# A third attention unit turned by DMA after GpSimd lays it apart, with values and a convolution step moved

## The chip, the core and the metric

The kernel runs on one core of one Trainium2 chip. Five engines work side by side there: PE (TensorE, matrix products and transposes by an identity), DVE (VectorE), ACT (ScalarE), POOL (GpSimd) and SP (SyncE, which issues most DMAs). Each engine takes its instructions in a fixed order and starts one when what it waits for is there. The metric is the device time of the whole program in microseconds (us), lower is better. The inputs lie in the device's main memory, and so does the output.

## The reference, cut to what matters

Two layers; in each, a feed-forward block, a mixing block and a second feed-forward block. The change lies in the mixing block alone.

```python
h = rms_norm(x, mix_norm[l])
z = h @ w_in[l]                                   # 512 x 2304
q, k, v = ...                                     # 8 query heads, 2 key/value heads of 64
attn_out = sliding_window_attention(q, k, v, attn_sink[l])
conv_out = short_conv(z[..., V_END:CB_END], z[..., CB_END:CC_END], z[..., CC_END:CH_END], conv_w[l])
x = x + jnp.concatenate([attn_out, conv_out], axis=-1) @ w_out[l]
```

Attention works on blocks of 128 tokens: a block of queries sees its own block of keys and the one before. `short_conv(b, c, h)` is `b * conv3(c * h)`, a causal convolution over three tokens in each of 512 channels.

## The kernel before

**Layout.** Activations lie transposed, features on the 128 partitions and the 512 tokens along the row. Every float32 operand of a product is split into a high part (`wh`, `xh`, `ph`: ACT casts it) and a low part (`wl`, `xl`, `pl`: DVE subtracts the high part from the whole), and a product is high·high + high·low + low·high. One product of 128 output features (`group`, lines 302 to 325) is 8 slabs of 128 input features with 3 matmuls each: L318 (`wh`,`xh`), L319 (`wh`,`xl`), L321 (`wl`,`xh`). The call `between(k, hi, lo)` ahead of slab k lets other work of PE be put inside.

**The mixing block.** After keys, values and queries come 12 products for the convolution, one for each `step` from 6 to 17, in two pairs of channel blocks: two for C (`cc`, L1700), two for the convolved input (`ch`, L1707, and then taps and sums), two for B (L1720). Each product is followed by `go_on()`, which runs `attend(step)` and then asks for the split of later weights (`need_split`), which the scheduler may not place ahead of the instruction `last` that `attend` returned.

**The attention units.** There are eight, 4 heads by 128 queries each: units 0 to 3 are token blocks 0 to 3 of the first key/value head, units 4 to 7 those of the second. In the traces' names a unit is `block_head`: unit 1 is `1_0`, unit 2 is `2_0`, unit 3 is `3_0`, unit 4 is `0_1`, unit 5 is `1_1`. A unit has three stages, and the tables `SCORES_AT`, `TURN_AT` and `VALUES_AT` (lines 56 to 60) give each unit's step for them:

- *scores*: 8 matmuls (L1554, L1555); DVE adds the bias and takes the maximum (L1558); DVE negates it (`nm`, L1569); ACT takes the exponential of each head (L1575, it needs `nm`); DVE scales by the reciprocal of the sum (L1583, four instructions). Unit 2's stand at step 7.
- *turn*: the probabilities `p` are turned so that keys lie on the partitions, and split into `ph` (ACT, L1621) and `pl` (DVE, L1622). Units 0, 2, 4, 6 and 7 are turned by PE: 4 transposes for each block of keys (L1616) into a PSUM tile `pt`. Units 1, 3 and 5 (`SEND_AT`) are turned by DMA: `send` has ACT lay the two 16-bit halves of each word apart in a room of their own (`crossing`, L1590), SP issues a transposing DMA (L1592), and later `join` has ACT put the halves together again (L1601), once for each block of keys.
- *values*: 2 matmuls for each block of keys (L1633, L1634), ACT copies half of the result (L1636), DVE adds (L1639).

`INSIDE = (11, 4, 5)` puts unit 4's turn (4 transposes, it has one block of keys) inside the product of step 11, ahead of slab 5.

**A convolution channel's end** (lines 1709 to 1716): ACT scales `ch` twice (`cc`, `tap`), DVE adds the third tap (L1712, inputs `ch` and `tap`, both in SBUF), POOL adds and multiplies (L1715, L1716). Then comes `go_on()`.

**What sets the order.** The lists above give the order of the calls; a scheduler places the instructions on each engine by its own costs, so that DVE's and ACT's order can shift far from the code. Tiles of p share 8 buffers with the raw weights (`stock`).

Of the kernel before, what the change touches and what calls it, by code (L numbers as in the profile page):

```python
# [14 lines left out]
ALU = mybir.AluOpType  # L15
# [3 lines left out]
S = 512  # L19
# [35 lines left out]
STREAM_BACK_AT = {9: 0, 11: 1, 16: 2, 18: 3}  # L55
SCORES_AT = (5, 6, 7, 8, 9, 10, 12, 13)

SEND_AT = {7: 1, 9: 3, 11: 5}
TURN_AT = (6, 9, 8, 11, 10, 13, 14, 15)
VALUES_AT = (7, 10, 9, 12, 11, 14, 15, 16)  # L60
INSIDE = (11, 4, 5)
WARM = 3
XT_TAGS = ("sc", "aux", "aux", "mm", "sc", "sc", "aux", "aux")

# [11 lines left out]
def trunk_kernel(  # L76
# [23 lines left out]
    nc = tc.nc  # L100
# [31 lines left out]
    def f32(ap):  # L132
        return ap.bitcast(F32)

    def words(ap):

        return ap.bitcast(U16).rearrange("p (n two) -> p two n", two=2)
# [50 lines left out]
    def conv_of(l, k, c):  # L188
        at = 48 + 12 * l + 4 * k + c
        return par[:, at : at + 1]  # L190
# [1303 lines left out]
    def mix(l, norm, after):  # L1494
        q = [None] * NH

        mixed = [g8(f"m_{l}_{j}", F32, (P, KC // 2, S)) for j in range(2)]
# [37 lines left out]
        class Unit:  # L1535
# [49 lines left out]
            def send(self):  # L1585


                self.room = crossing[:, todo.index(self) // 2 % 2, :]
                halves = self.room.bitcast(U16).rearrange("p (two n) -> p two n", two=2)
                nc.scalar.copy(halves, words(self.p.rearrange("p h k -> p (h k)")))  # L1590
                self.turned = self.p.rearrange("p h k -> p (h k)").bitcast(U16)
                nc.sync.dma_start_transpose(  # L1592
                    self.turned.rearrange("p (c q) -> p c q", q=P),
                    halves.rearrange("p two n -> p (two n)"),
                )
# [11 lines left out]
            def turn(self):  # L1607

                self.pt = []
                for kb in range(self.lo // P, 2):  # L1610
                    if todo.index(self) in SEND_AT.values():
                        tp = self.join(kb)
                    else:
                        tp = psum("aux", [P, 4, P], f"pt_{self.name}_{kb}")
                        for h in range(4):
                            nc.tensor.transpose(  # L1616
                                tp[:, h, :], self.p[:, h, kb * P : (kb + 1) * P], ident
                            )
                    hi = g2(f"ph_{self.name}_{kb}", F32R, (P, 4, P))
                    lo = g2(f"pl_{self.name}_{kb}", F32R, (P, 4, P))  # L1620
                    nc.scalar.copy(hi, tp)  # L1621
                    last = nc.vector.tensor_sub(lo, tp, f32(hi))  # L1622
                    self.pt.append((kb, hi, lo))
                return last

# [17 lines left out]
        todo = [Unit(n, g) for g in range(NKV) for n in range(NT)]  # L1643
        crossing = g8(f"crossing_{l}", F32, (P, 2, 4 * 2 * P))

        def attend(step):

            done = None
            if step in SEND_AT:
                todo[SEND_AT[step]].send()  # L1650
            for at, stage in ((VALUES_AT, "values"), (TURN_AT, "turn"), (SCORES_AT, "scores")):
                if stage == "turn" and step + 1 == INSIDE[0]:
                    done = todo[VALUES_AT.index(step)].added
                    continue
                if step in at:
                    done = getattr(todo[at.index(step)], stage)() or done
            return done

        for j in range(NH // 2):
# [16 lines left out]
        step = 6  # L1676

        def product():

            def between(k, hi, lo):  # L1680
                if step == INSIDE[0] and k == INSIDE[2]:
                    todo[INSIDE[1]].turn()

            return group(norm.h, between, own=take_split(SPLIT_AHEAD - 1))

# [10 lines left out]
        for pair in range(2):  # L1696
            cs = []
            for j in range(2):
                c = g2(f"cc_{l}_{pair}_{j}")
                nc.vector.tensor_mul(c, product(), inv2)  # L1700
                cs.append(c)
                go_on()
            ys = []
            for j in range(2):
                c = 2 * pair + j
                u = g2(f"ch_{l}_{pair}_{j}")
                nc.vector.tensor_mul(u, product(), cs[j])  # L1707
                y = cs[j]
                nc.scalar.activation(y, u, AF.Copy, scale=conv_of(l, 2, c))
                tap = g2(f"tap_{l}_{c}")  # L1710
                nc.scalar.activation(tap[:, 1:], u[:, : S - 1], AF.Copy, scale=conv_of(l, 1, c))
                nc.vector.scalar_tensor_tensor(  # L1712
                    tap[:, 2:], u[:, : S - 2], conv_of(l, 0, c), tap[:, 2:], op0=ALU.mult, op1=ALU.add
                )
                nc.gpsimd.tensor_add(y[:, 1:], y[:, 1:], tap[:, 1:])  # L1715
                nc.gpsimd.tensor_mul(y, y, norm.inv)  # L1716
                ys.append(y)
                go_on()
            for j in range(2):
                last = nc.vector.tensor_mul(mixed[1][:, 2 * pair + j, :], product(), ys[j])  # L1720
                go_on()
                if step == 17:
                    with tc.issue_after(state["turned"]):
                        ops.make("b11")
# [60 lines left out]
```

## Time and profile before

| | |
|---|---|
| time, median of 3 runs | 1626.22 us (1626.18 to 1626.57) |
| the profiled execution, its own time | 1626.19 us |
| its span, first to last instruction | 1624.4 us |
| PE busy | 1615.4 us (99%) |
| DVE busy | 1376.7 us (85%) |
| ACT busy | 1178.1 us (73%) |
| POOL busy | 216.5 us (13%) |
| steps 6 to 12 of the first layer's mixing block | 368.6 to 416.6 us of the span |
| the same stretch of the second layer | 1171.4 to 1219.3 us |

The profile is one execution. Its page gives busy times and the chain of work that ended last; views of the trace give instructions in order of time (start, length, engine, line, what is written and read, and in brackets how long the engine stood idle before it and what ended that), groups of instructions, and who waited for whom. PE counts as busy from the start of one matmul to the modelled end of the last that overlaps it, so its waits are best read from the distance of one start to the next: 0.227 us between products of 512 columns that wait for nothing. Instructions on ACT and DVE overlap too: the next starts about 0.1 us before the end of the one before.

### The profile page before, as it was taken

What the parts mean: (1) busy time and instruction counts of PE and PEld (TensorE: products, weight loads), DVE (VectorE), ACT (ScalarE), POOL (GpSimd) and SP (SyncE); (2) the same over time, 40 slices, a digit from 0 to 9 for tenths busy, and PEclk for the clock granted to TensorE, in tenths of its full rate; (3) what the DMA queues carried; (4) which work ended last, traced back from release to release, by engine and by line L of the source; (5) the groups of instructions that cost most, each with busy time, mean ns of one, the idle gap of its engine ahead of it and who ended that gap; (6) DMA issues with size and microseconds to landing.
All of it is one profiled execution on the core that took longest, in us unless ns stands there. A gap on an engine that the chain in (4) does not pass through costs nothing.

```text
span 1624.4 us, 21158 instructions
## 1 busy us (share of the span) xinstructions
PE 1615.4 (99%) x7571; PEld 1349.4 (83%) x7571; DVE 1376.7 (85%) x1788; ACT 1178.1 (73%) x1511; POOL 216.5 (13%) x191
## 2 busy tenths in 40 slices
PE   9999999999999999999999999999999999999998
PEld 7888888888898888888888888888888988888887
DVE  7978798988899977798998777989688998678997
ACT  6677777857766677778866777788586767878665
POOL 1211111001211111111011111110012111111121
PEclk9999999999999999999999999999999999999999
DMA  9999989822597698999767999998136978999892
GB/s 270 212 232 209 220 207 226 233 59 78 143 227 175 177 225 214 218 214 225 218 144 182 224 215 226 215 221 217 42 91 156 233 149 219 225 223 222 241 230 72
DMA packets 306031, 313.92 MB, mean 193 GB/s; under 512 B 125501, under 2 KB 188549, under 8 KB 305925
## 3 DMA queue, kind: packets, MB, share of 16 engines
q1 hardware_dynamic: 265412, 230.90, 50.1%
q0 software_dynamic: 40048, 81.27, 29.3%
q8 instruction: 59, 0.97, 0.2%
q14 instruction: 48, 0.39, 0.1%
q10 hardware_dynamic: 464, 0.40, 0.1%
HBM read 264.29 MB, written 2.10 MB: 164 GB/s over the span
## 4 chain that ended last, share of the span: by engine, by line
PE 98%; DVE 1%; DMA 0%; SPq 0%; issue 0%; ACT 0%; DVEq 0%
PE x L842 27%; PE y L842 13%; PE x_s L842 9%; PE acc L318 7%; PE acc L319 7%; PE acc L321 7%; PE w L842 7%; PE y_s L842 5%; PE x_m L827 3%; PE w_s L842 3%; PE y_m L827 1%; PE y_e L842 1%; PE acc L699 1%; PE x_e L842 1%; PE w_m L827 1%; PE sc L1555 0%
## 5 line engine op out<-in xcount | busy, mean ns | idle before, releaser
L228 DVE TENSOR_TENSOR wl<-raw,wh 128x1024 fp32r<-128x1024 f32 (+1 forms) x494 | 598.6, 1219 | 162.8 <-ACT wh L228 161.9
L228 ACT CAST wh<-raw 128x1024 fp32r<-128x1024 f32 (+1 forms) x494 | 514.1, 1044 | 304.6 <-PE x L842 92.8
L318 PE MATMUL acc<-xh,wh 128*128 128x512 f32 x392 | 153.3, 393 | 0.5 <-ACT wh L228 0.5
L319 PE MATMUL acc<-xl,wh 128*128 128x512 f32 x392 | 153.1, 391 | 0.0
L321 PE MATMUL acc<-xh,wl 128*128 128x512 f32 x384 | 149.7, 390 | 0.0
L223 POOL DMA_DIRECT2D raw<-in_ffn_wu_dram x40 | 50.6, 1272 | 381.6 <-DMA raw<-in_ffn_wu_dram 268.6
L318 PEld LDWEIGHTS acc<-xh,wh 128*128 128x128 f32 x392 | 73.8, 188 | 15.0 <-ACT wh L228 0.6
L319 PEld LDWEIGHTS acc<-xl,wh 128*128 128x128 f32 x392 | 73.7, 188 | 14.5
L321 PEld LDWEIGHTS acc<-xh,wl 128*128 128x128 f32 x384 | 72.1, 188 | 15.3
L223 POOL DMA_DIRECT2D raw<-in_ffn_wd_dram x34 | 41.0, 1218 | 272.0 <-DMA raw<-in_ffn_wd_dram 122.3
L223 POOL DMA_DIRECT2D raw<-in_ffn_wg_dram x40 | 49.1, 1237 | 201.9 <-DMA raw<-in_ffn_wu_dram 84.7
L269 DVE TENSOR_TENSOR raw<-raw,raw 128x1024 f32<-128x1024 f32 x58 | 70.5, 1220 | 1.7 <-DMA raw<-in_ffn_wu_dram 1.2
L1106 ACT COPY raw_a<-turned 128x1024 uint16<-128x1024 uint16 x48 | 63.5, 1357 | 0.0
L842 PE MATMUL x<-wl,ft1h 128*128 128x512 f32 x160 | 62.4, 390 | 0.0
L842 PE MATMUL w<-wh,fb21h 128*128 128x512 f32 x160 | 62.3, 390 | 0.0
L842 PE MATMUL y<-wh,ft3h 128*128 128x512 f32 x160 | 62.3, 390 | 0.0
L842 PE MATMUL x<-wh,ft1l 128*128 128x512 f32 x160 | 62.3, 389 | 0.0
L842 PE MATMUL x<-wl,ft2h 128*128 128x512 f32 x160 | 62.3, 389 | 0.0
L842 PE MATMUL x<-wh,ft2l 128*128 128x512 f32 x160 | 62.3, 389 | 0.0
L842 PE MATMUL x<-wh,ft1h 128*128 128x512 f32 x160 | 62.3, 389 | 0.0
L842 PE MATMUL w<-wh,fb21l 128*128 128x512 f32 x160 | 62.2, 389 | 0.0
L842 PE MATMUL y<-wh,ft3l 128*128 128x512 f32 x160 | 62.2, 389 | 0.0
(517 smaller groups left out, 4545.2 us busy)
## 6 DMA issues: line engine op xcount, KB each, us to landing
raw<-in_ffn_wu_dram SPq DMA_DIRECT2D x127, 512.0 KB, 5.6
raw<-in_ffn_wd_dram SPq DMA_DIRECT2D x105, 512.0 KB, 5.6
raw<-in_ffn_wg_dram SPq DMA_DIRECT2D x86, 512.0 KB, 5.3
raw<-in_ffn_wu_dram POOLq DMA_DIRECT2D x40, 512.0 KB, 9.1
raw<-in_ffn_wg_dram POOLq DMA_DIRECT2D x40, 512.0 KB, 6.5
raw<-in_w_in_dram SPq DMA_DIRECT2D x36, 512.0 KB, 4.0
raw<-in_ffn_wd_dram POOLq DMA_DIRECT2D x34, 512.0 KB, 8.2
raw<-in_w_out_dram SPq DMA_DIRECT2D x20, 512.0 KB, 4.6
```

Source lines behind the costliest of these rows:

```text
L223: nc.gpsimd.dma_start(out=r, in_=rows_of(*more), accum_op=ALU.add)
L228: return nc.scalar.copy(hi, raw), eng.tensor_sub(lo, raw, f32(hi))
L269: nc.vector.tensor_add(a11, a11, s1)
L318: nc.tensor.matmul(acc, hi[:, k, :], rhs[k][0], start=k == first, stop=False)
L319: nc.tensor.matmul(acc, hi[:, k, :], rhs[k][1], start=False, stop=False)
L321: nc.tensor.matmul(acc, lo[:, k, :], rhs[k][0], start=False, stop=k == last)
L699: nc.tensor.matmul(opening[n], (lo if part == "w" else hi)[:, k, :], xl if part == "x" else xh, start=n not in begun, stop=k == KC - 1 and ...
L827: nc.tensor.matmul(accs[c // 2][:, c % 2, :], w[:, k, cols], x_[:, 2 * h + k, :], start=start and c % 2 == 0 and h + k + i == 0, stop=h + ...
L842: nc.tensor.matmul(accs[u], x_[:, 2 * h + k, tok], w[:, k, :], start=start and h + k + i == 0, stop=h + k == 2 and i == 2, skip_group_chec ...
L1106: nc.scalar.copy(words(raws[self.b][:, c, :]), self.to[:, :, c, :])
```

## The change

Unit 2 is turned by DMA too, and its two halves are laid apart by POOL instead of ACT, into the half of `mixed[1]` that is not yet in use. Its turn moves from step 8 to step 10 and its values from step 9 to step 11. Unit 1's values move from the end of step 10 into the product of step 11, ahead of slab 3. At step 9 (the second channel of the first pair) `go_on()` comes ahead of DVE's third tap, and this tap may not stand ahead of unit 1's last `pl`. Where a stage stands inside a product, `attend` now returns unit 1's last `pl` as `last`. Step 6 and everything outside the mixing block stay as they are.

```diff
-SEND_AT = {7: 1, 9: 3, 11: 5}
-TURN_AT = (6, 9, 8, 11, 10, 13, 14, 15)
-VALUES_AT = (7, 10, 9, 12, 11, 14, 15, 16)
-INSIDE = (11, 4, 5)
+SEND_AT = {7: 1, 8: 2, 9: 3, 11: 5}
+TURN_AT = (6, 9, 10, 11, 10, 13, 14, 15)
+VALUES_AT = (7, None, 11, 12, 11, 14, 15, 16)
+INSIDE = {(11, 3): (1, "values"), (11, 5): (4, "turn")}
+Y_BEHIND = {9: 1}
+IDLE_LAYS = (2,)
...
-                self.room = crossing[:, todo.index(self) // 2 % 2, :]
+                n = todo.index(self)
+                self.room = crossing[:, n // 2 % 2, :]
+                if n == 2:
+                    self.room = mixed[1][:, 2:4, :].rearrange("p c s -> p (c s)")
...
-                nc.scalar.copy(halves, words(self.p.rearrange("p h k -> p (h k)")))
+                whole = words(self.p.rearrange("p h k -> p (h k)"))
+                (nc.gpsimd.tensor_copy if n in IDLE_LAYS else nc.scalar.copy)(halves, whole)
...
-                    last = nc.vector.tensor_sub(lo, tp, f32(hi))
+                    last = self.parted = nc.vector.tensor_sub(lo, tp, f32(hi))
...
-                if stage == "turn" and step + 1 == INSIDE[0]:
-                    done = todo[VALUES_AT.index(step)].added
-                    continue
-                if step in at:
-                    done = getattr(todo[at.index(step)], stage)() or done
+                for n in (n for n, when in enumerate(at) if when == step):
+                    if (n, stage) in INSIDE.values():
+                        done = todo[1].parted
+                    else:
+                        done = getattr(todo[n], stage)() or done
...
-                if step == INSIDE[0] and k == INSIDE[2]:
-                    todo[INSIDE[1]].turn()
+                if (step, k) in INSIDE:
+                    n, stage = INSIDE[step, k]
+                    getattr(todo[n], stage)()
...
-                nc.vector.scalar_tensor_tensor(
-                    tap[:, 2:], u[:, : S - 2], conv_of(l, 0, c), tap[:, 2:], op0=ALU.mult, op1=ALU.add
-                )
+                ys.append(y)
+                unit = Y_BEHIND.get(step)
+                if unit is not None:
+                    go_on()
+                with tc.issue_after(todo[unit].parted.ins) if unit is not None else nullcontext():
+                    nc.vector.scalar_tensor_tensor(
+                        tap[:, 2:], u[:, : S - 2], conv_of(l, 0, c), tap[:, 2:], op0=ALU.mult, op1=ALU.add
+                    )
                 nc.gpsimd.tensor_add(y[:, 1:], y[:, 1:], tap[:, 1:])
                 nc.gpsimd.tensor_mul(y, y, norm.inv)
-                ys.append(y)
-                go_on()
+                if unit is None:
+                    go_on()
```

Three places show how the instructions move; the other layer's rows read alike. In the changed kernel line numbers are 2 to 12 higher.

DVE, from unit 2's scaling on, before (`p_2_0` is unit 2's scaling by the sums, `ISA` rows are the biased maxima of unit 3, `tap_0` the third tap of channel block 0, `nm_3_0` the negated maximum that unit 3's exponentials need):

```order
L1583 TENSOR_SCALAR p_2_0_3357<-p_2_0_3357,sums_2_0_3376 128x256 x4
L1558 ISA p_3_0_3446,mx_3_0_3445<-sc_3_0_0_3447,bias,sink 128x256
L1558 ISA mx_3_0_3445 128x1
L1558 ISA p_3_0_3446,mx_3_0_3445<-sc_3_0_1_3454,bias,sink 128x256
L1558 ISA mx_3_0_3445 128x1
L1712 SCALAR_TENSOR_TENSOR tap_0_3422<-ch_0_0_3394,par,tap_0_3422 128x510
L1622 TENSOR_TENSOR pl_2_0_0_3433<-pt_2_0_0_3427,ph_2_0_0_3432 128x512
L1558 ISA p_3_0_3446,mx_3_0_3445<-sc_3_0_1_3454,bias,sink 128x256
L1558 ISA mx_3_0_3445 128x1
L1622 TENSOR_TENSOR pl_2_0_1_3442<-pt_2_0_1_3436,ph_2_0_1_3441 128x512
L1569 TENSOR_SCALAR nm_3_0_3461<-mx_3_0_3445 128x4
```

and in the changed kernel, first on DVE, then POOL's part of the same time:

```order
L1585 TENSOR_SCALAR p_2_0_3357<-p_2_0_3357,sums_2_0_3376 128x256 x4
L1724 SCALAR_TENSOR_TENSOR tap_0_3422<-ch_0_0_3394,par,tap_0_3422 128x510
L1560 ISA p_3_0_3430,mx_3_0_3429<-sc_3_0_1_3438,bias,sink 128x256
L1560 ISA mx_3_0_3429 128x1
L1571 TENSOR_SCALAR nm_3_0_3445<-mx_3_0_3429 128x4
L1573 TENSOR_TENSOR es_3_0_3447<-sink,nm_3_0_3445 128x4
L1714 TENSOR_TENSOR ch_0_1_3467<-acc_3468,cc_0_1_3320 128x512
```

```order
L1596 COPY m_1_2959<-p_2_0_3357 128x2048
L1727 TENSOR_TENSOR cc_0_0_3246<-cc_0_0_3246,tap_0_3422 128x511
L1728 TENSOR_TENSOR cc_0_0_3246<-cc_0_0_3246,inv_3011 128x512
L1727 TENSOR_TENSOR cc_0_1_3320<-cc_0_1_3320,tap_1_3495 128x511
L1728 TENSOR_TENSOR cc_0_1_3320<-cc_0_1_3320,inv_3011 128x512
```

The two `pl` of unit 2 have left this place, three of unit 3's four maxima now stand ahead of the scaling, and `nm_3_0` comes three rows behind it. POOL's copy is new and is the first thing that POOL does after the scaling.

ACT, from the exponentials of unit 3 to the first rows of unit 2's joining, in the changed kernel (`wh` casts are weights of later products, L1596 is unit 3's laying apart, L1607 a joining); before, the stretch from unit 3's exponentials to unit 1's second `ph` was the second fence:

```order
L1577 ACTIVATE p_3_0_3430,sums_3_0_3449<-p_3_0_3430,nm_3_0_3445 128x256 x4
L1580 ACTIVATE es_3_0_3447<-es_3_0_3447 128x4
L230 CAST wh_3620<-raw_3314 128x1024
L1716 ACTIVATE cc_0_1_3320<-ch_0_1_3467,par 128x512
L1718 ACTIVATE tap_1_3495<-ch_0_1_3467,par 128x511
L1596 COPY crossing_3080<-p_3_0_3430 128x2048
L1627 CAST ph_1_0_0_3500<-crossing_3080 128x512
L1577 ACTIVATE p_0_1_3510,sums_0_1_3529<-p_0_1_3510,nm_0_1_3525 128x128
L1627 CAST ph_1_0_1_3505<-crossing_3080 128x512
L1577 ACTIVATE p_0_1_3510,sums_0_1_3529<-p_0_1_3510,nm_0_1_3525 128x128 x3
L1580 ACTIVATE es_0_1_3527<-es_0_1_3527 128x4
L1607 COPY m_1_2959<-p_2_0_3357 128x2x512 x2
```

```order
L1575 ACTIVATE p_3_0_3446,sums_3_0_3465<-p_3_0_3446,nm_3_0_3461 128x256 x4
L1578 ACTIVATE es_3_0_3463<-es_3_0_3463 128x4
L1709 ACTIVATE cc_0_1_3320<-ch_0_1_3483,par 128x512
L1711 ACTIVATE tap_1_3511<-ch_0_1_3483,par 128x511
L1636 COPY ol_2_0_3523<-o_2_0_3518 64x512
L1621 CAST ph_1_0_0_3528<-crossing_3080 128x512
L1590 COPY crossing_3080<-p_3_0_3446 128x2048
L1621 CAST ph_1_0_1_3533<-crossing_3080 128x512
```

Unit 3's laying apart moved ahead of unit 1's first `ph`, a weights' cast came in, unit 2's `ol` copy left, and two joinings follow.

DVE ahead of the low weights of step 11's product (`wl_3544`; before, `wl_3572`) in the changed kernel, and PE in that product:

```order
L1628 TENSOR_TENSOR pl_1_0_0_3501<-crossing_3080,ph_1_0_0_3500 128x512
L1628 TENSOR_TENSOR pl_1_0_1_3506<-crossing_3080,ph_1_0_1_3505 128x512
L230 TENSOR_TENSOR wl_3544<-raw_3164,wh_3543 128x1024
L1581 TENSOR_TENSOR sums_0_1_3529<-sums_0_1_3529,es_0_1_3527 128x4
L1724 SCALAR_TENSOR_TENSOR tap_1_3495<-ch_0_1_3467,par,tap_1_3495 128x510
```

```order
L323 MATMUL acc_3624<-xh_2_2932,wl_3544 128x512
L1639 MATMUL o_1_0_3634<-ph_1_0_0_3500,vv_3202 128x512
L1640 MATMUL o_1_0_3634<-pl_1_0_0_3501,vv_3202 128x512
L1639 MATMUL o_1_0_3634<-ph_1_0_1_3505,vv_3202 128x512
L1640 MATMUL o_1_0_3634<-pl_1_0_1_3506,vv_3202 128x512
L320 MATMUL acc_3624<-xh_2_2932,wh_3543 128x512
```

In the kernel before, `wl_3572` stood behind the same `pl` rows and these four values stood ahead of the product; unit 2's four stood ahead of step 10's.

## The prediction

> **What bounds the kernel now.** First the page's span, busy times and chain of work that ended last:
>
> ```profile
> span 1624.4 us, 21158 instructions
> PE 1615.4 (99%) x7571; PEld 1349.4 (83%) x7571; DVE 1376.7 (85%) x1788; ACT 1178.1 (73%) x1511; POOL 216.5 (13%) x191
> PE 98%; DVE 1%; DMA 0%; SPq 0%; issue 0%; ACT 0%; DVEq 0%
> ```
>
> PE's own work is 98% of the chain. A change gains what it takes off PE and loses what it makes PE wait. Second, the view of waits for PE over the whole run, its last row:
>
> ```profile
> PE acc L318 <- ACT wh L228: 0.5, 1, 0.5
> ```
>
> So there is next to no waiting to win back, and no idle time on PE that could swallow a new wait. Third, busy times by engine in steps 7 to 12 of the first layer (stretch, length, then PE, PEld, DVE, ACT, POOL):
>
> ```profile
> 375.20:416.60 41.40, 41.40 (x206) 34.36 (x205) 35.69 (x114) 34.59 (x74) 5.51 (x4) 1.00 0.33 89
> ```
>
> ACT and DVE are 84% and 86% busy there, more than ACT's 73% over the run: these two are the next in line, and the change touches the orders of both.
>
> **What it takes off PE.** The timeline of PE at unit 2's transposes, its values, unit 1's values and the head of step 11's product (start, length, line):
>
> ```profile
> 389.57 0.40 PE L318 MATMUL acc<-xh,wh 128*128 128x512 f32 x1
> 389.81 1.12 PE L1616 MATMUL pt<-ident,p 128*128 128x128 f32 x8
> 391.01 0.39 PE L321 MATMUL acc<-xh,wl 128*128 128x512 f32 x1
> 395.32 0.39 PE L1633 MATMUL o<-ph,vv 128*128 128x512 f32 x1
> 396.23 0.22 PE L1554 MATMUL sc<-kh,q 128*128 128x128 f32 x1
> 402.62 0.39 PE L1633 MATMUL o<-ph,vv 128*128 128x512 f32 x1
> 403.08 0.39 PE L1633 MATMUL o<-ph,vv 128*128 128x512 f32 x1
> 403.43 0.50 PE L1634 MATMUL o<-pl,vv 128*128 128x512 f32 x1
> 403.76 0.28 PE L1554 MATMUL sc<-kh,q 128*128 128x256 f32 x1
> 405.19 0.39 PE L321 MATMUL acc<-xh,wl 128*128 128x512 f32 x1
> ```
>
> From L318 to L321 in step 9 are 1.44 us; two products without the transposes take 2 x 0.23 = 0.46. The eight transposes are worth 0.98 us a layer. Unit 1's last two values are 0.35 and 0.33 us apart from what follows instead of 0.23, so they wait for some 0.2 us; this goes too. The eight values themselves only move. **Gain: 1.2 us a layer.**
>
> They move behind the head of step 11's product, though. Its first matmul on low weights (L321 at 405.19) comes earlier by the transposes (0.98), unit 2's values (396.23 - 395.32 = 0.91) and unit 1's (403.76 - 402.62 = 1.14): PE wants these low weights at **402.2**, 3.0 us before it did. Are they there?
>
> **The low weights of step 11.** DVE makes them (`wl`) right behind unit 1's second `pl`, which needs unit 1's second `ph` from ACT, which in ACT's new order stands behind unit 3's exponentials, a weights' cast, a channel's two scalings and unit 3's laying apart. The exponentials need `nm`, and `nm` now stands behind POOL's copy. What a POOL instruction does to DVE shows in the timelines of both:
>
> ```profile
> 393.74 1.29 POOL L1716 TENSOR_TENSOR cc<-cc,inv 128x512 f32<-128x512 f32 x1
> 394.40 0.66 DVE L1569 TENSOR_SCALAR nm<-mx 128x4 f32<-128x4 f32 x1
> 399.82 1.29 POOL L1715 TENSOR_TENSOR cc<-cc,tap 128x511 f32<-128x511 f32 x1 [4.79 <-issue]
> 400.48 1.18 DVE L1622 TENSOR_TENSOR pl<-crossing,ph 128x512 fp32r<-128x512 f32 x1
> 401.19 1.63 POOL L1716 TENSOR_TENSOR cc<-cc,inv 128x512 f32<-128x512 f32 x1
> 402.40 0.97 DVE L1622 TENSOR_TENSOR pl<-crossing,ph 128x512 fp32r<-128x512 f32 x1
> 393.80 0.69 DVE L1622 TENSOR_TENSOR pl<-pt,ph 128x512 fp32r<-128x512 f32 x1 [0.57 <-ACT ph L1621]
> L1569 DVE TENSOR_SCALAR nm<-mx x16: 154/170/657, 372.2 to 1232.6; 128x4 f32<-128x4 f32 x16
> ```
>
> `nm` takes 0.17 us at the median (the last row: shortest, median and longest in ns), but 0.66 beside POOL, and it ends at 395.06, POOL at 395.03. The `pl` that read SBUF alone end at 401.66 and 403.37, 0.55 us behind POOL's ends at 401.11 and 402.82; the one that reads PSUM (393.80) keeps its 0.69. So a DVE instruction on SBUF waits until the whole POOL instruction is over. `nm` does too.
>
> How long POOL's copy of 2048 elements takes is not in this trace. The nearest rows, POOL's and ACT's own laying apart:
>
> ```profile
> 0.88 0.21 POOL L171 MEMSET ones<- 128x128 f32 x1
> 1.36 0.29 POOL L173 CAST ones_r<-ones 128x128 fp32r<-128x128 f32 x1
> 1.59 0.10 POOL L441 MEMSET eps<- 128x1 f32 x1
> 399.53 1.90 ACT L1590 COPY crossing<-p 128x2048 uint16<-128x2048 uint16 x1
> ```
>
> Below: ACT's 1.90, and the memsets agree ((0.21 - 0.10) / 127 = 0.87 ns an element, 1.9 us). Above: the two-input instruction of 1.29 us for 512, so 5.2 us for 2048. Nearest is the cast, one input and one output: (0.29 - 0.10) / 127 = 1.5 ns an element, so 0.1 + 3.1 = **3.2 us**.
>
> The Trainium skill, GPSIMD Engine Reference, Engine selection, says that an instruction with one input runs roughly at line rate there. At the clock of 1.2 GHz on the same page an estimate is 2048 / 1.2 = 1.7 us; the sum then would be that of the short copy below. The cast's row speaks against it.
>
> Now the chain in the first layer, with these rows of DVE and ACT:
>
> ```profile
> 389.19 1.13 DVE L1583 TENSOR_SCALAR p<-p,sums 128x256 f32<-128x256 f32 x4
> 390.25 0.47 DVE L1558 CUSTOM_DVE_ANT_0 p<-sc,bias,sink 128x256 f32<-128x256 f32 x1
> 391.48 0.75 DVE L1712 SCALAR_TENSOR_TENSOR tap<-ch,par,tap 128x510 f32<-128x510 f32 x1 [0.34 <-ACT tap L1711]
> 394.98 1.21 DVE L228 TENSOR_TENSOR wl<-raw,wh 128x1024 fp32r<-128x1024 f32 x1
> 388.89 1.37 ACT L1601 COPY crossing<-p 128x1024 uint16<-128x1024 uint16 x1
> 390.12 0.71 ACT L1709 ACTIVATE cc<-ch,par 128x512 f32<-128x512 f32 x1
> 395.10 0.51 ACT L1575 ACTIVATE p<-p,nm 128x256 f32<-128x256 f32 x1 [1.33 <-DVE nm L1569]
> 395.61 0.49 ACT L1575 ACTIVATE p<-p,nm 128x256 f32<-128x256 f32 x1
> 401.33 0.62 ACT L1621 CAST ph<-crossing 128x512 fp32r<-128x512 f32 x1
> 401.85 1.99 ACT L228 CAST wh<-raw 128x1024 fp32r<-128x1024 f32 x2
> 403.75 0.40 ACT L1575 ACTIVATE p<-p,nm 128x128 f32<-128x128 f32 x1
> ```
>
> - Unit 2's scaling ended at 390.3; two maxima of 0.40 us now go ahead of it: 391.1. The tap follows, to 391.8 (it reads SBUF twice, so POOL waits for it), POOL's copy runs to **395.0**. `nm`, due at 392.2, ends with it.
> - ACT would be free for unit 3's exponentials at 393.5 (`cc` and `tap` at 388.9 and 389.5, two joinings of 1.23 start to start, a cast of 0.95). It waits until 395.0. Then, start to start: four exponentials 4 x 0.49 and one of 0.10, cast 0.95, two scalings 0.62 each, laying apart 1.80, `ph` 0.52, exponential 0.40, `ph` 0.62 to its end: 7.6 us, so 402.6.
> - DVE: `pl` 0.6, `wl` 1.2: low weights at **404.4**. PE wants them at 402.2. **Loss: 2.2 us.** Without the hold ACT starts at 393.5 and the loss is 0.7; beyond 1.7 us each microsecond of copying costs one.
>
> **The low part of unit 4.** PE goes on at 404.4 with 22 of the product's matmuls (5.0), unit 1's four values (0.9), unit 4's transposes (0.4), unit 2's values (0.9) and one of unit 4's (0.2), and wants unit 4's `pl` at 411.8. On ACT, behind 402.6: the rest of the exponentials 1.2, joining of unit 2 2 x 1.23, `ph` 0.5, a joining of unit 3 1.23, `ph` of unit 2 until 408.5. On DVE the two POOL instructions of the second channel, which the change moves to about 405 to 408, hold unit 4's scalings in the same way, so unit 2's two `pl` (0.6 each) and two maxima (0.4 each) only end at about 410.0. Two more maxima 0.8, `wl` of the next product 1.1, `nm` and unit 1's sums 0.9 stand ahead of unit 4's `pl` (0.7): 413.4 or so. **Loss: 1.5 us**; without POOL's holds about 0.6.
>
> **What hides the rest.** Unit 2's DMA: issued at 395.0, landed by the slowest of these 5.2 us later, wanted by ACT only at about 403.8; its cover is 3.6 us.
>
> ```profile
> DMA to landing us min/median/max: 3.6/3.7/5.2
> raw<-in_w_in_dram SPq DMA_DIRECT2D x6, 512.0 KB, 4.0
> ```
>
> On SP one load of `w_in` now stands behind two transposing DMAs and starts some 8 us later, near 404. It lands 4.0 us later, and step 13's casts want it past 413. Both cost nothing. Without its cover a late turn would cost PE as much as it is late, since unit 2's values stand in PE's row. Behind step 12 the order is the old one.
>
> **Sum.** A layer: -1.2 + 2.2 + 1.5 = +2.5 us. Both layers have the same orders: +5.0. The profiled execution took 1626.19 us, 0.03 under the median of 1626.22, and its span 1624.4. So 1626.2 + 5.0 = **1631.2 us**.
>
> **The rivals.**
> - *The short copy.* POOL copies in 1.9 us, as ACT does. The Trainium skill's rule above would make it so. The first loss falls from 2.2 to 0.9, a layer to +1.2: 1628.6 us. For it: the memsets' slope. Against it: the cast's. Chance 0.18.
> - *The long copy.* POOL copies at its two-input rate, 5.2 us. The first loss grows by 2.0 us a layer: 1635.2. For it: 16-bit elements taken from every second place, for which no POOL row exists. Above 6.6 us the DMA's cover of 3.6 is used up as well. Chance 0.14.
> - *PE waits for nothing new.* Copy and DVE don't hold each other, and ACT runs ahead of my sum by the 0.7 us that remain. Then the gain stands: 1626.2 - 2.4 = 1623.8. With the holds gone but ACT's order as it is, losses of 0.7 + 0.6 leave +0.1 a layer, 1626.4. It decides as soon as `nm` keeps its 0.17 us beside the copy. For it: three held instructions are little evidence, and none stood beside a one-input copy. Against it: the two `pl` end the same 0.55 us behind POOL, and `nm` 0.03. The 1626.4 is also the case in which the change doesn't do what it says: the transposes go, and the new order takes the time back. Chance of both 0.14.
>
> **How the numbers follow.** Forecast 0.52, with a range of its own from 1629 to 1633.5 (copy of 2.3 to 4.2 us), then 0.18, 0.14, 0.14, and 0.02 for things unseen. 0.2% of 1626.2 is 3.25 us, about what a measurement of this kernel can tell from no change: below 1623.0 is faster, above 1629.5 slower. PE can win 2.4 us at most, so faster has 0.02. Within 0.2% are the third rival, most of the short copy and a little of the forecast: 0.14 + 0.12 + 0.03 = 0.29. Slower: 0.69. The range takes in short and long copy: 1626.8 to 1636.0.
>
> **What would show it.** In the changed kernel's trace: a POOL copy (L1596) of some 3.2 us, and `nm` of unit 3 beside it, 2 us long or more and ending with it; in the view of waits for PE two new rows in each layer, low weights (`acc` behind `wl`) of about 2 us in step 11 and `o` behind `pl` of about 1.5 at its end; 48 transposes at L1622 instead of 64; unit 3's exponentials starting near 395.0. The prediction is wrong if `nm` keeps 0.17 us beside the copy, if the copy is under 2 us, or if PE's waits in steps 9 to 12 stay under 1.2 us a layer.

## The result, and the profile after

The changed kernel takes 1630.26 us (median of 10 runs, 1629.59 to 1631.22), the kernel before 1626.37 us beside it (10 runs, 1625.96 to 1626.90). The ratio is 1.0024, with a 95% interval from 1.0014 to 1.0033: 3.9 us more, or 1.95 us a layer. The page's first lines, and its chain of work that ended last:

```profile
span 1627.8 us, 21135 instructions
PE 1613.5 (99%) x7555; PEld 1347.4 (83%) x7555; DVE 1383.2 (85%) x1788; ACT 1182.8 (73%) x1515; POOL 220.4 (14%) x193
PE 95%; DVE 3%; ACT 1%; issue 0%; DMA 0%; SPq 0%; DVEq 0%; ACTq 0%
```

PE has 16 matmuls fewer and is 1.9 us less busy, but the chain is no longer 98% PE: DVE has 3% of it. Where, the view of waits for PE says (total in us, times, longest):

```profile
PE o L1640 <- DVE pl L1628: 3.4, 2, 1.7
PE acc L323 <- DVE wl L230: 1.7, 2, 0.9
```

Both rows are new and each stands once in each layer. In the timeline of PE the wait is read from the distance of two starts, less the 0.227 us of a product that waits for nothing:

```profile
401.82 0.40 PE L321 MATMUL acc<-xl,wh 128*128 128x512 f32 x1
403.07 0.50 PE L323 MATMUL acc<-xh,wl 128*128 128x512 f32 x1 [0.85 <-DVE wl L230]
403.41 0.40 PE L320 MATMUL acc<-xh,wh 128*128 128x512 f32 x1
...
410.53 0.39 PE L1639 MATMUL o<-ph,vv 128*128 128x512 f32 x1
412.60 0.50 PE L1640 MATMUL o<-pl,vv 128*128 128x512 f32 x1 [1.68 <-DVE pl L1628]
```

At the head of step 11's product PE loses 1.25 - 0.23 = 1.02 us, and 0.11 more because the next start is 0.34 behind; at unit 4's low part 2.07 - 0.23 = 1.84, and 0.10 more in the same way. Together 3.1 us a layer, against the 1.2 that the change takes off PE: 1.9. What the other engines did there (timelines of POOL, then DVE, then ACT of the changed kernel):

```profile
391.25 2.27 POOL L1596 COPY m<-p 128x2048 uint16<-128x2048 uint16 x1 [45.26 <-DVE p L1585]
393.49 1.28 POOL L1727 TENSOR_TENSOR cc<-cc,tap 128x511 f32<-128x511 f32 x1
403.92 1.30 POOL L1727 TENSOR_TENSOR cc<-cc,tap 128x511 f32<-128x511 f32 x1 [7.78 <-DVE sums L1582]
405.30 1.35 POOL L1728 TENSOR_TENSOR cc<-cc,inv 128x512 f32<-128x512 f32 x1
...
391.03 0.74 DVE L1724 SCALAR_TENSOR_TENSOR tap<-ch,par,tap 128x510 f32<-128x510 f32 x1
392.21 1.34 DVE L1571 TENSOR_SCALAR nm<-mx 128x4 f32<-128x4 f32 x1
393.59 1.20 DVE L1573 TENSOR_TENSOR es<-sink,nm 128x4 f32<-128x4 f32 x1
401.79 1.22 DVE L230 TENSOR_TENSOR wl<-raw,wh 128x1024 fp32r<-128x1024 f32 x1
404.32 2.61 DVE L1585 TENSOR_SCALAR p<-p,sums 128x128 f32<-128x128 f32 x4
411.85 0.69 DVE L1628 TENSOR_TENSOR pl<-pt,ph 128x512 fp32r<-128x512 f32 x1
...
392.43 1.04 ACT L230 CAST wh<-raw 128x1024 fp32r<-128x1024 f32 x1
393.59 0.51 ACT L1577 ACTIVATE p<-p,nm 128x256 f32<-128x256 f32 x1
397.85 1.88 ACT L1596 COPY crossing<-p 128x2048 uint16<-128x2048 uint16 x1
```

`nm`, 0.17 us otherwise, takes 1.34 and ends at 393.55, with POOL's copy (393.52); `es` then ends with POOL's next instruction. Unit 4's four scalings take 2.61 us beside POOL's pair and end soon after it (406.93, the pair at 406.65). But ACT's cast, which stands ahead of the exponentials, only ends at 393.47, so the exponentials lose only some 0.2 us to the hold of `nm`. The Trainium skill (SBUF — State Buffer, Who interferes with whom) says that DVE and GpSimd share a pair of ports as an exclusive lock, which the first to issue keeps for its whole instruction where DVE needs that pair; these rows agree, `nm` and `es` ending within 0.03 us of POOL's instructions.

### The profile page after: what moved, and what is told of

Same layout as the page of the kernel before. It is cut to its first block, busy times and chain, and to the rows that moved or that the text cites. A ratio compares the mean times of both kernels' runs of the same rounds, so it can differ in the third digit from the quotient of the medians.

```text
span 1627.8 us, 21135 instructions
## 1 busy us (share of the span) xinstructions
PE 1613.5 (99%) x7555; PEld 1347.4 (83%) x7555; DVE 1383.2 (85%) x1788; ACT 1182.8 (73%) x1515; POOL 220.4 (14%) x193
## 4 chain that ended last, share of the span: by engine, by line
PE 95%; DVE 3%; ACT 1%; issue 0%; DMA 0%; SPq 0%; DVEq 0%; ACTq 0%
PE x L844 27%; PE y L844 13%; PE x_s L844 9%; PE w L844 7%; PE acc L320 7%; PE acc L321 7%; PE acc L323 6%; PE y_s L844 5%; PE w_s L844 3%; PE x_m L829 3%; PE y_m L829 1%; PE y_e L844 1%; PE acc L701 1%; PE x_e L844 1%; PE w_m L829 1%; DVE wl L230 1%
## 5 line engine op out<-in xcount | busy, mean ns | idle before, releaser
L844 PE MATMUL x<-wl,fb11h 128*128 128x512 f32 x160 | 62.2, 389 | 0.0
L844 PE MATMUL w<-wl,fb21h 128*128 128x512 f32 x160 | 62.2, 389 | 0.0
```

The lines of the kernel that those rows point to most:

```text
L844: nc.tensor.matmul(accs[u], x_[:, 2 * h + k, tok], w[:, k, :], start=start and h + k + i == 0, stop=h + k == 2 and i == 2, skip_group_chec ...
```

## The experiments

Each run stands beside the kernel before (1626.4 us). Where nothing else is said, waits are those of the view of waits for PE, which counts both layers. Runs in which something is left out compute something else; they are there for their times alone.

| run | us, median | ratio to before, 95% |
|---|---|---|
| the tap at once | 1631.14 | 1.0019 to 1.0041 |
| POOL's pair left out | 1628.17 | 1.0002 to 1.0021 |
| ACT lays unit 2 apart | 1632.75 | 1.0024 to 1.0053 |
| POOL copies twice | 1632.62 | 1.0024 to 1.0054 |
| unit 1's values alone | 1628.74 | 1.0004 to 1.0023 |
| the DMA turn alone | 1628.84 | 1.0006 to 1.0025 |
| unit 3 laid apart late | 1629.13 | 1.0006 to 1.0025 |
| the same, unit 4 later | 1630.09 | 1.0013 to 1.0032 |
| the added work left out | 1629.48 | 1.0012 to 1.0030 |
| late, later, work left out | 1628.83 | 1.0003 to 1.0022 |
| a version to beat both | 1629.77 | 1.0010 to 1.0028 |
| unit 5's turn left out too | 1624.79 | 0.9981 to 1.0000 |

**The second wait: POOL's pair beside unit 4's scalings.** Two runs take the pair away, by leaving it out and by putting it back.

```diff
-                nc.gpsimd.tensor_add(y[:, 1:], y[:, 1:], tap[:, 1:])
-                nc.gpsimd.tensor_mul(y, y, norm.inv)
+                if unit is None:
+                    nc.gpsimd.tensor_add(y[:, 1:], y[:, 1:], tap[:, 1:])
+                    nc.gpsimd.tensor_mul(y, y, norm.inv)
```

> POOL's add and multiply at the end of the second convolution channel of the first pair are left out (that channel lacks its taps and its norm), DVE's order around it stays row for row. Theory (POOL's two instructions hold unit 4's scalings, and these delay unit 4's pl): the four scalings go from 2.61 us back to some 0.9, and the wait of o behind pl falls from 1.85 us by 0.9 to 1.7; the wait of acc behind wl keeps its 1.0 us. Some 1627.3 to 1628.5 us. Rival A (unit 4's pl is late because of ACT's order alone): scalings end earlier, pl does not, the time stays within 0.5 us of 1630.3.

From its timeline of DVE and its waits:

```profile
404.48 0.87 DVE L1585 TENSOR_SCALAR p<-p,sums 128x128 f32<-128x128 f32 x4
...
PE acc L323 <- DVE wl L230: 1.7, 2, 0.8
PE o L1640 <- DVE pl L1628: 1.1, 2, 0.5
```

The scalings are back at 0.87 us, the wait at `pl` falls from 3.4 to 1.1, the other stays at 1.7, and 2.1 of the 3.9 us are gone. POOL's pair made most of the second wait. The other way:

```diff
-Y_BEHIND = {9: 1}
+Y_BEHIND = {}
```

> The third tap and its two POOL instructions go back to their old place at step 9; the DMA turn and the moved values stay. Theory (PE waits twice a layer because ACT's new order and POOL's instructions make DVE late, and the second wait comes from POOL's two instructions beside unit 4's scalings): the scalings go back from 2.6 to 0.9 us and the wait of o behind pl at the end of step 11 (1.85 us a layer) falls under 0.3; tap and POOL now stand ahead of unit 1's pl again, so the wait of acc behind wl grows from 1.0 to some 2 to 2.4 us. Net 0.4 to 0.7 us a layer less than the changed kernel, some 1629.2 us. Rival A (the second wait comes from ACT's two more joinings, the tap's place does not matter): the wait of o behind pl keeps its 1.7 to 2.1 us and the time stays at 1630.3. Rival B (the tap's move is what costs): both waits go and the time falls to some 1624 to 1626.

```profile
PE acc L323 <- DVE wl L230: 3.8, 2, 1.9
```

Its only wait in the mixing block over 0.4 us is the first one, twice as long as it was: the pair now holds `nm` of unit 4 and unit 1's `pl`. So far as expected; the time is not (1631.1, not 1629.2). In the second layer PE's clock halved behind the wait, in the first it did not. The windows of this run in the second layer (stretch, length, busy PE, PEld, DVE, ACT, POOL, granted clock, DMA share, GB/s):

```profile
1210.00:1212.00 2.00, 2.00 (x6) 1.54 (x6) 2.00 (x9) 2.00 (x3) 0.00 (x0) 0.50 0.88 249
1212.00:1214.00 2.00, 2.00 (x9) 1.56 (x8) 2.00 (x8) 2.00 (x3) 0.00 (x0) 0.78 0.78 227
```

The profiled execution took 1630.2 us and has one such stretch and a mean granted clock of 0.998; five of the seven took 1631.1 us or more at 0.997, the mean clock that the next run's profile shows with two stretches. So the median run probably lost time to the clock in both layers; no trace of it was kept.

**POOL's copy.** Doubled, and given to ACT:

```diff
                 (nc.gpsimd.tensor_copy if n in IDLE_LAYS else nc.scalar.copy)(halves, whole)
+                if n in IDLE_LAYS:
+                    nc.gpsimd.tensor_copy(halves, whole)
```

> POOL copies unit 2's halves twice (the same result), all else as in the changed kernel. Theory (DVE's nm waits for the whole POOL instruction and the exponentials of unit 3 for nm; with one copy the exponentials start when ACT is free, so a second copy costs its whole length): nm ends with the second copy near 395.8, the exponentials start 2.2 us later, the wait of acc behind wl grows from 1.0 to 2.8 to 3.3 us; the second wait stays at 1.6 to 2.0. 1633.5 to 1634.7 us. Should DVE slip its nm between the two copies, nm ends near 393.5 as now, es takes the hold, and the time stays near 1630.3: then it is the single instruction, not POOL's busy time, that holds. Rival (no hold reaches PE; ACT's order alone sets the low weights): the time stays near 1630.3 with nm at the end of the second copy, since the exponentials' delay is absorbed.

POOL's timeline, one row of DVE's and one of ACT's:

```profile
391.45 2.26 POOL L1596 COPY m<-p 128x2048 uint16<-128x2048 uint16 x1 [45.28 <-DVE p L1585]
393.68 1.28 POOL L1729 TENSOR_TENSOR cc<-cc,tap 128x511 f32<-128x511 f32 x1
394.90 1.89 POOL L1598 COPY m<-p 128x2048 uint16<-128x2048 uint16 x1
396.75 1.30 POOL L1730 TENSOR_TENSOR cc<-cc,inv 128x512 f32<-128x512 f32 x1
...
397.25 1.75 DVE L1585 TENSOR_SCALAR p<-p,sums 128x256 f32<-128x256 f32 x4
...
399.02 1.90 ACT L1596 COPY crossing<-p 128x2048 uint16<-128x2048 uint16 x1 [0.90 <-DVE p L1585]
```

The scheduler put the add between the copies, so `nm` was held by the first alone. The second cost by another road: it pushed the multiply onto unit 3's scalings (1.75 us, 1.14 in the changed kernel), and ACT waited 0.90 us for them. The first wait grew by 1.0 us a layer. The second fell to 0.2, though `pl` came no sooner (413.70, against 412.54 in the changed kernel): PE had become late, by the longer wait, and by running at half clock behind it (0.427 us between products), as its timeline shows.

```profile
404.27 0.50 PE L323 MATMUL acc<-xh,wl 128*128 128x512 f32 x1 [1.86 <-DVE wl L230]
...
406.69 0.63 PE L1642 MATMUL o<-pl,vv 128*128 128x512 f32 x1
407.12 0.63 PE L1641 MATMUL o<-ph,vv 128*128 128x512 f32 x1
```

None of the three cases of the expectation came out whole. The copy's own time did: 1.89 us where nothing is in its way; the 2.26 holds some 0.4 of waiting behind DVE's tap.

```diff
-IDLE_LAYS = (2,)
+IDLE_LAYS = ()
```

> ACT lays unit 2's halves apart instead of POOL (the same room), all else as in the changed kernel. Theory (both engines are full here; POOL's copy costs the exponentials only some 0.2 us since ACT is busy until 393.4 anyway): nm falls from 1.34 to some 0.2 to 0.7 us, but ACT does 1.9 us more, so the low weights of step 11 come no earlier; the waits of PE in steps 9 to 12 sum to 2.3 to 3.2 us a layer as now (2.9) and the time stays within 1 us of 1630.3. Rival (the forecast's first loss: the hold of nm by POOL's copy is most of it): the wait of acc behind wl falls to 0.3 us or less and the time to some 1628.3 us. Rival B (POOL's copy is the saving that makes the change bearable): waits grow by the whole 1.9 us a layer, 1634.

```profile
PE acc L323 <- DVE wl L230: 4.2, 5, 1.2
PE acc L320 <- DVE m L1645: 2.3, 2, 1.2
```

The profiled execution took 1635.8 us, 3.0 above the median, and began the mixing block 1.4 us later than the changed kernel's, so its waits are not all those of the median. The first wait is a little longer (1.49 us from start to start), and new ones follow it. By the medians the run takes 2.5 us more than the changed kernel: neither "the same" nor the whole 3.8. POOL's copy saves more than it holds up. On the hold of `nm` the run says little: `nm` is held here too (1.02 us, beside POOL's add, which now comes first), but ACT is busy with the laying apart meanwhile.

**One part alone.** In the first, unit 2 stays with PE; in the second, unit 1's values and the tap stay where they were. (The tables are those of the changed kernel but for these.)

```diff
# unit 1's values alone
+SEND_AT = {7: 1, 9: 3, 11: 5}
+TURN_AT = (6, 9, 8, 11, 10, 13, 14, 15)
+VALUES_AT = (7, None, 9, 12, 11, 14, 15, 16)
+Y_BEHIND = {}
# the DMA turn alone
+VALUES_AT = (7, 10, 11, 12, 11, 14, 15, 16)
+INSIDE = {(11, 5): (4, "turn")}
+Y_BEHIND = {}
```

> One part alone: unit 1's values inside the product of step 11; unit 2 is turned by PE at step 8 as before, its values at step 9, the tap in its old place. Theory (DVE makes the low weights of step 11 only behind unit 1's pl, and PE now wants them 1.1 us sooner): new waits of 0.7 to 1.4 us a layer in steps 11 and 12 (acc behind wl some 0.4, o behind ph or pl of unit 4 some 0.7), 1627.8 to 1629.2 us. Rival (the move costs nothing where unit 2 stays with PE): no wait above 0.3 us, 1626 us.

> One part alone: unit 2 laid apart by POOL, turned by DMA at step 10, its values at step 11; unit 1's values stay behind step 10, the tap in its old place. Theory (PE gets to unit 1's values 1.9 us sooner, 0.98 for the transposes and 0.91 for unit 2's values, and ACT and DVE do not have unit 1's pl ready): a wait of o behind pl of 1.2 to 1.7 us a layer at step 10, the rest under 0.6, 1627.9 to 1629.5 us. Rival (the DMA turn by itself pays, the moved values and the moved tap are what cost): no wait above 0.3 us, 1624.0 to 1625.0 us.

Waits of the first (two rows), then of the second:

```profile
PE o L1639 <- ACT ph L1627: 1.0, 2, 0.5
PE acc L323 <- DVE wl L230: 0.8, 2, 0.4
...
PE o L1640 <- DVE pl L1628: 2.6, 2, 1.3
```

Each loses some 2.4 us by itself, and the largest waits are at the places expected. (In the second the row is 1.46 us a layer from start to start; some 0.9 more lies in waits of 0.1 to 0.2 us that the view doesn't list.) Neither part is the culprit alone: each lets PE come sooner, and PE then finds something not ready.

**The first wait: ACT's order.** ACT may lay unit 3 apart only behind unit 1's second `ph` (`high`); for that, `send` is called behind the turn of its step:

```diff
-            if step in SEND_AT:
-                todo[SEND_AT[step]].send()
...
+                if stage == "turn" and step in SEND_AT:
+                    todo[SEND_AT[step]].send()
...
-                    nc.scalar.copy(hi, tp)
+                    self.high = nc.scalar.copy(hi, tp)
...
-                (nc.gpsimd.tensor_copy if n in IDLE_LAYS else nc.scalar.copy)(halves, whole)
+                with tc.issue_after(todo[1].high.ins) if n == 3 else nullcontext():
+                    (nc.gpsimd.tensor_copy if n in IDLE_LAYS else nc.scalar.copy)(halves, whole)
```

> As the changed kernel, but ACT may lay unit 3 apart only behind unit 1's second ph (1.9 us of ACT leave the way ahead of it). Theory (the first wait comes from ACT's order, not from the hold of nm): the wait of acc behind wl falls from 1.0 to under 0.3 us; but the work is only moved, and PE, now 1 us earlier, finds unit 4's scaled probabilities late: a new wait of 1.3 to 1.9 us a layer at its transposes (pt), o behind pl under 0.5. 1628.0 to 1629.6 us. Rival A (the hold of nm by POOL's copy makes the first wait): acc behind wl keeps 0.8 us or more, 1630.3 or above. Rival B (the second wait is a matter of its own): acc behind wl goes, o behind pl keeps its 1.85 or grows by 1.0.

```profile
PE pt L1623 <- DVE p L1585: 3.0, 2, 1.5
```

The first wait is gone, with POOL's copy and the hold of `nm` still there: ACT's order made it. As foreseen the wait turns up again, at unit 4's transposes, and 1.1 us of the 3.9 are saved. Then unit 4 was put off as well:

```diff
+TURN_AT = (6, 9, 10, 11, 11, 13, 14, 15)
+VALUES_AT = (7, None, 11, 12, 13, 14, 15, 16)
+INSIDE = {(11, 3): (1, "values"), (12, 5): (4, "turn")}
```

> As the kernel before it in this list, and unit 4's transposes move on to the product of step 12, ahead of slab 5, its values behind step 13: PE asks for unit 4 more than a step later. Theory (ACT and DVE have too little room in steps 9 to 13; whatever PE no longer waits for, it waits for the next thing): the wait at pt goes, but acc behind wl of step 12 and o behind ph or pl of unit 2 take 1.2 to 2.0 us a layer together, 1627.6 to 1629.0 us. Rival (unit 4's early date is the only obstacle): no wait above 0.3 us in steps 9 to 13 and 1623.8 to 1624.6 us, faster than before.

```profile
PE o L1641 <- DVE pl L1629: 1.3, 4, 0.4
PE acc L323 <- DVE wl L230: 1.1, 2, 0.6
PE o L1640 <- ACT ph L1628: 0.9, 2, 0.5
```

The wait at the low weights of step 12 came as expected. The waits of `o` did not: unit 2's values (from 408.31 us) wait for nothing, unit 3's, at 417 us, wait for `ph` and for `pl`, and a further one came at 446 us. The time, 1630.1, was above the range given.

**The added work, or the order?** Unit 2's laying apart, DMA and joining are left out, first in the changed kernel's order, then in that of the run before:

```diff
-SEND_AT = {7: 1, 8: 2, 9: 3, 11: 5}
+SEND_AT = {7: 1, 9: 3, 11: 5}
...
-                whole = self.room[:, kb * 4 * P : (kb + 1) * 4 * P]
+                room = crossing[:, 0, :] if todo.index(self) in IDLE_LAYS else self.room
+                whole = room[:, kb * 4 * P : (kb + 1) * 4 * P]
+                if todo.index(self) in IDLE_LAYS:
+                    return whole.rearrange("p (h q) -> p h q", h=4)
```

> The changed kernel's tables and order, but all work that the change adds is left out: POOL does not lay unit 2 apart, no DMA turns it, ACT does not join it; its high and low parts are made from unit 1's turned probabilities instead (unit 2's attention is left out). Theory (the new order of DVE and ACT alone makes PE wait; POOL's copy costs the exponentials 0.2 us and ACT's joinings nothing): acc behind wl keeps 0.7 to 1.0 us a layer, o behind pl 1.6 to 1.9, 1629.4 to 1630.3 us. Rival A (the forecast's view, that the hold of nm by POOL's copy sets the low weights): acc behind wl falls under 0.3 us, o behind pl grows by as much or stays, 1628.3 or the same. Rival B (ACT's two joinings of 2.6 us a layer set both waits): both waits fall under 0.4 us and the time to some 1624.5 us.

Its waits, and `nm` in its timeline of DVE:

```profile
PE o L1643 <- DVE pl L1631: 3.5, 2, 1.8
PE acc L323 <- DVE wl L230: 1.3, 2, 0.6
...
392.28 1.02 DVE L1571 TENSOR_SCALAR nm<-mx 128x4 f32<-128x4 f32 x1
```

With nothing of the added work done, 3.0 of the 3.9 us remain, and both waits with them (0.80 and 1.93 us from start to start, 1.02 and 1.84 in the changed kernel): the order alone makes most of the loss. (`nm` is held all the same: where the copy is gone, POOL's add comes sooner and holds it.)

> The same work left out, in the order of the run with unit 3's laying apart behind unit 1's ph and unit 4's transposes in step 12, its values behind step 13, which measured 1630.1 us with the work in it. Theory (with that order what PE waits for is the room that ACT lacks: POOL's copy and ACT's joinings are what fills it): no wait above 0.4 us in steps 9 to 13, 1624.4 to 1625.6 us, so 4.5 to 5.7 us less than with the work. Rival (order again: the added work is hidden there too): 1629 us or more, with waits at wl of step 12 and at unit 2's o.

This expectation fell: 1628.8 us, not some 1625. Its one larger wait row is

```profile
PE o L1644 <- DVE pl L1632: 1.7, 5, 0.5
```

of which, in the first layer's timeline, one stands at 416 us and the others near 437 and 446, in the values of units 6 and 7; in the second layer there are two, at 1221 and 1250. So there was a limit farther on. Rows of ACT at unit 5's joining in the first layer in the kernel before, and in this run at the same place with the first exponential of unit 6, then the joining in the second layer:

```profile
420.66 2.57 ACT L1601 COPY crossing<-p 128x1024 uint16<-128x1024 uint16 x2 [2.40 <-DMA p<-crossing]
```

```profile
420.69 2.55 ACT L1611 COPY crossing<-p 128x1024 uint16<-128x1024 uint16 x2 [2.88 <-DMA p<-crossing]
423.11 0.50 ACT L1577 ACTIVATE p<-p,nm 128x256 f32<-128x256 f32 x1
...
1223.52 2.56 ACT L1611 COPY crossing<-p 128x1024 uint16<-128x1024 uint16 x2 [1.08 <-DMA p<-crossing]
```

In the first layer the joining stands at the same time to 0.03 us, though PE starts the next product 0.7 us sooner: ACT sits and waits for unit 5's DMA, and unit 6 queues behind it. That DMA takes 5.2 us to land there, in the kernel before as well; in the second layer it lands after 3.6 and 3.7 us, ACT waits only 1.1 us in this run, and the waits of PE behind it are shorter. Why the first layer's lands so late is open: in the changed kernel none took more than 3.7. The last kernel takes this away too (`SEND_AT = {7: 1, 9: 3}`, `IDLE_LAYS = (2, 5)`):

> As the run in which unit 3 is laid apart late, unit 4 is wanted later and unit 2's added work is left out (1628.8 us); now unit 5 too is neither laid apart nor turned by DMA nor joined, its parts are made from unit 1's turned probabilities (unit 5's attention is left out as well). Theory (in that run PE is 1.4 us ahead of the kernel before at 416 us, and gives it back because ACT sits 2.9 us before unit 5's joining until the DMA lands at 420.7, no sooner than before, and the exponentials of units 6 and 7 queue behind it): the waits of o behind pl near 437 and 446 us fall under 0.3 us and the time to 1624.0 to 1626.6 us. Rival (the last units are late for DVE's order of its own): these waits keep 0.5 us or more each, 1628.0 us or above.

Its waits of `o`, the same exponential, and the first product behind attention (`x_m`) here, and in the run before:

```profile
PE o L1644 <- DVE pl L1632: 0.9, 2, 0.5
...
420.29 0.51 ACT L1577 ACTIVATE p<-p,nm 128x256 f32<-128x256 f32 x1 [2.72 <-DVE nm L1571]
...
L829 PE MATMUL x_m<-fb11h_m,wh x32: 278/284/284, 450.9 to 1258.2; 128*128 128x256 f32 x32
```

```profile
L829 PE MATMUL x_m<-fb11h_m,wh x32: 278/284/284, 453.1 to 1261.6; 128*128 128x256 f32 x32
```

Unit 6 starts 2.8 us sooner, the waits near 437 and 446 are gone (the 0.9 is that at 416 in each layer), and the time is 1624.79 us, 1.6 under the kernel before (the interval just reaches no change), of the 2.4 that the transposes and the small wait are worth. Unit 5's way through laying apart, DMA and joining was the next limit. Of the 3.4 us by which `x_m` comes sooner at the end, 2.2 are won in the first layer, where the DMA had landed late, and 1.2 in the second. Which of the three steps counts most, this run doesn't tell apart; ACT's idle 2.9 us before the first layer's joining point to the transfer there.

**A version to beat both.** It leaves nothing out: unit 3 laid apart late, units 2 and 4 later, the tap behind unit 4's scalings:

```diff
+TURN_AT = (6, 9, 11, 11, 11, 13, 14, 15)
+VALUES_AT = (7, None, 12, 12, 13, 14, 15, 16)
+INSIDE = {(11, 3): (1, "values"), (12, 5): (4, "turn")}
...
-                with tc.issue_after(todo[unit].parted.ins) if unit is not None else nullcontext():
+                with tc.issue_after(todo[4].scaled.ins) if unit is not None else nullcontext():
```

> A version meant to beat both: the changed kernel with unit 3 laid apart behind unit 1's ph, unit 2's turn and values one step later (11 and 12), unit 4's transposes in step 12 and its values behind step 13, and the second channel's tap and POOL's two instructions behind unit 4's scalings, so that they hold none of them. Theory (each of the waits seen so far loses its cause, ACT's load stays): waits of 0.3 to 1.2 us a layer are left, 1625.0 to 1628.0 us. Rival (ACT's room is what is short, and any order pays it): 1.2 to 2 us of waits a layer turn up, some of them behind step 13, and the time is 1628.5 to 1630.5.

```profile
PE o L1641 <- DVE pl L1629: 2.2, 4, 0.6
```

The rival held: no wait of note is left before 414 us, but behind it two in each layer, near 415 and 445 us in the first, and the time is 1629.8 us. (The profiled execution took 1628.6; the eleven lie between 1628.2 and 1631.0.) No kernel of these that leaves nothing out beat the one before.

## Why the prediction was right, and where its sizes were off

The time fell inside the range, 0.9 us under the forecast, and 0.24% slower, on the side that the likeliest case named. The mechanism held: work came off PE, ACT and DVE in their new orders came too late twice a layer, and POOL's instructions held DVE's. That the time came so near is in part luck, since the first loss was put too high and the second too low. By its steps:

- **The gain.** Step 11's low weights are wanted at 401.82 + 0.23 = 402.05; the prediction said 402.2. Right.
- **POOL's copy** was the term that was mis-sized: 3.2 us taken from the cast's row, where its own time is 1.89 (0.92 ns an element, near the memsets' 0.87 and far from the cast's 1.5). The 2.27 of its row hold some 0.4 of waiting behind the tap, which the prediction had too. So it ended at 393.5, not 395.0. With 1.9 us for the copy the prediction's own sum gives 1628.6, 1.7 under what was measured.
- **The hold** of `nm` until the end of POOL's instruction was right, 393.55 beside 393.52. Its price was not: ACT is busy until 393.47 (393.5 in the prediction), so the hold costs some 0.2 us where 1.5 was expected.
- **The first loss**: 1.1 us, not 2.2. ACT's new order alone, 0.7 us in the prediction, is most of it: laying unit 3 apart late removes it with the hold still there, and leaving out the copy leaves 0.80 of 1.02.
- **The second loss**: 1.95 us, not 1.5. The forecast had PE want unit 4's `pl` at 411.8 and get it at 413.4, which is 1.6 and not 1.5; it was 410.76 and 412.54. Since the first loss was smaller, PE came 1.0 us sooner, and DVE only 0.9. That POOL's pair makes the larger part, and that some 0.6 us would remain without it, the run without the pair bore out: 0.69 us from start to start less 0.227.
- **What hides the rest.** Unit 2's DMA was issued at 393.55 and landed 3.7 us later at the most, its joining began at 402.3; the load of `w_in` went out at 403.04. Nothing waits for either, as said.
- **The sum**: -1.2 + 1.1 + 1.95 = +1.85 us a layer, where +2.5 was forecast. The span grew by 3.4 us, the median by 3.9.
- **The rivals.** The short copy had the right price for the copy and the first loss (0.9), but not for the second. The rival in which POOL and DVE don't hold each other is out. Its side case, that the new order takes the gain back by itself, came nearest to the cause, though not to the time: it put 0.1 us a layer where the run without the added work, whose `nm` and scalings are still held, lost 1.5.
- "Behind step 12 the order is the old one" hid a limit: unit 5's DMA, which the kernel before waits for on ACT as well, with no cost to PE.
- **Its signs.** The 48 transposes and the two rows of waits in each layer came (1.0 and 1.84 us for "about 2" and "about 1.5"). Unit 3's exponentials began at 393.59, not near 395.0, `nm` took 1.34 us, not 2, and the copy's own time is under the 2 us that the prediction had named as a sign of being wrong. On the copy and its price it was wrong.

On the copy, the Trainium skill (GPSIMD Engine Reference, Engine selection) says that an instruction with one input goes roughly at line rate; the estimate of 1.7 us from that page's clock is nearer to the 1.89 measured than the 3.2 from the cast's row was.

## What to carry to other kernels

A kernel whose PE is 98% of the chain can still have its softmax chain just in time behind it: work taken off PE then pays only as far as the chain that feeds it can run ahead, so look first for the next place at which an engine of that chain sits and waits (here ACT, for a DMA) and ask whether that wait ends sooner too. In these runs an instruction on GpSimd cost what it held on VectorE at its own moment, not its length: price it by the instruction beside it and by whether that one was on time to begin with. And when a wait disappears, read PE's row on to the end of the stage before counting it as gained.

## What the runs showed of the hardware that was not expected

A wait of PE can cost twice. Waits of 1.84 to 1.93 us from start to start, less 0.227 (the changed kernel's second wait and that of the run without the added work, four cases) left the clock at 1.00. Of four waits of 2.02 to 2.05 us (POOL's copy twice, and the tap at once, two layers each) three were followed, 1.4 to 1.9 us later, by about 3.4 us in which the granted clock was 0.50 and products stood 0.427 us apart: some 1.6 us more each, nearly as much as the wait. The fourth, of 2.05 us, was not, so the length of the wait does not decide it alone. Nor is 1.93 shown to be safe: three of the ten executions without the added work took 1631.1 to 1631.5 us, the others at most 1629.8, and two of the three show a mean clock of 0.998, where the others show 0.999 or 1.000; their traces were not kept. The Trainium skill (TensorE: Matmul & The Clock Gate, HAM oscillation — how this bites in real kernels) gives the rule of no idle gaps of PE over some 3.4 us; here 2.0 us were enough in three cases of four, and the slow stretch is about as long as that figure.
